# Keeping only the second parts of weight blocks in DRAM, with fewer steps in a layer norm and moved feed points, in a two-layer trunk on one core

## The chip, the cores and the metric

The kernel runs on one core of a Trainium2 chip. The metric is the device time of one execution in microseconds (us). The kernel before took 2473.21 us, the median of 3 runs (2469.9 to 2479.39).

## The reference

One inference step of a decoder trunk of two layers, for a prompt of 256 tokens and 8 samples of 4 tokens, 288 token columns in all, which share the weights. The model width is 2048. Cut to what is computed:

```python
for l in range(2):
    a = _rms(h, norm_mix_pre[l])
    if l % 2 == 0:   # pooling mixer | retention mixer, one input and one output projection
        y, ph, rs = _even_mixer(a, pos0, pool_hist[i], ret_state[i], w_in_even[i], w_pool[i],
                                s_pool[i], w_out_even[i])
    else:            # spatial gating mixer | Conformer convolution
        y, ch, sv = _odd_mixer(a, conv_hist[i], w_in_odd[i], sg_ln_g[i], sg_ln_b[i], sg_w[i], sg_b[i],
                               dw_w[i], dw_b[i], cv_ln_g[i], cv_ln_b[i], w_out_odd[i])
    h = h + _rms(y, norm_mix_post[l])
    f = _rms(h, norm_ffn_pre[l])
    f = jnp.square(jax.nn.relu(f @ w_up[l])) @ w_down[l]
    h = h + _rms(f, norm_ffn_post[l])
```

In the odd layer the four quarters of `a @ w_in` are u, v, a and gate. `v` takes a gelu and a layer norm, is mixed along the tokens and multiplied with gelu(u); `a * sigmoid(gate)` goes through a depthwise convolution of 31 taps, a second layer norm (`cv_ln`) and a silu. Both halves enter `w_out_odd`. Everything is float32; the outputs are the trunk's result for both groups and the new states.

## The kernel before

**Subs and groups.** Tokens lie along the free axis (288 columns), channels on partitions. All weights are streamed once, in 720 pieces of 256 rows by 512 columns, called subs (512 KB each, tile `raw`). A group is 512 output columns: 16 k-tiles in 8 subs (4 subs in the halves of `w_out_odd`). A group accumulates in four PSUM banks (`mm`). To keep float32 precision at the speed of a rounded type, each operand is split in two: ScalarE (ACT) rounds `raw` to `whi`, VectorE (DVE) computes `wlo = raw - whi`, and TensorE (PE) does three matmuls for each product: `whi` with the high part of the activations (`xhi`, `hidhi`), `wlo` with the same, and `whi` with their low part (`xlo`, `hidlo`). So a sub is 24 matmuls of 128x128 by 288 columns.

**The stages, in order of time.** Layer 0: the input projection of the even layer and its output projection (`wo_e`), up to 437 us; the MLP, to 1268 us, in four quarters of `up0` (4 groups) and `dn0` (4 groups). Layer 1: `w_in_odd` in eight groups in the order ga0, ga1, ga2, v0, v1, ga3, u0, u1 (ga: a and gate, together) from 1268 to 1506 us; `w_out_odd` in two halves (wo0, wo1) to 1640 us; the second MLP (`up1`, `dn1`) to the end.

**The feed.** Every sub takes a place in a list `feed`; `run()` (line 651) walks the subs, and at each emits what lets the next ones arrive: `emit_dma` loads `raw` (4 buffers) on the SP queue, `emit_hi` is the ACT rounding, `emit_lo` the DVE subtraction, each in a ring of `RING` = 3 pairs (`whi`, `wlo`) and some extra ones. `some(2)` lets two more places of the feed be split per sub. Every engine executes its instructions in the order in which they are emitted, so a `wlo` that waits for its `whi` holds up all that DVE has behind it. SP issues DMAs in order too.

**Kept subs.** In the MLP of layer 0 some places of the feed are jobs: a job loads, rounds and subtracts a sub of a later stage, in a pair of the same ring, and writes both parts to DRAM (`hik`, `lok`). The later sub is then of kind "kept" and reads both parts by DMA, with no work on ACT or DVE. `JOBS = (1, 5)` places two jobs in each group of the MLP but the first and the last. Sixty subs are kept: all 8 of ga0, 4 of each of the other seven groups of `w_in_odd`, 16 of `w_out_odd`, 8 of the first group of `up1`. `plan()` (line 537) pairs jobs and kept subs.

**Between the stages.** `boundary()` (line 371) closes a root mean square norm and opens the next: `last_sums` adds up squares on PE (`ms`), POOL and DVE make the factor (`sm`), PE spreads it over the partitions, `grow` scales `y` and adds it to `h`, and `xhi`, `xlo` are made from `h`. `keep_warm(n)` issues n matmuls whose result nobody reads. In the first group after a boundary the matmuls are ordered with k outside (`kouter`), and its results are parked (`defer`) until the norm's factor `rb` is there (`rest()`, line 689).

**Work beside the odd layer's matmuls.** The convolution runs in the background: taps on DVE (`cacc`), on ACT with a sum on POOL (`tap`, `conv`), one `bg_step` for each sub. When it is done, `conv_out` (line 1477) does the layer norm of the convolution (`layer_norm(..., by_pe=True)`, line 1342) and the silu, one step of the generator per sub, and makes `hidhi`, `hidlo` for the second half of `w_out_odd`. What is read out of PSUM at a group's end (`tmp<-mm`, `u<-mm`, `y<-mm`) stands in DVE's or ACT's order like all the rest, and PE needs these banks for the group after.

Of the kernel before, what the change touches and what calls it, by code (L numbers as in the profile page):

```python
# [178 lines left out]
def build(tc, ctx, I, O, C):  # L179
# [231 lines left out]
    def last_tiles(src, m):  # L411
# [61 lines left out]
    feed, pos, nraw, parts, kept = [], [], [], {}, {}  # L473
    RAW, RING = 4, 3
    JOBS = (1, 5)
# [16 lines left out]
    def emit_dma(p):  # L492
        kind, i = feed[p]
        if kind == "kept":
            return
# [16 lines left out]
    def emit_hi(p):  # L512
        kind, i = feed[p]
        hi, lo = parts[p] = ring_slot()
        if kind == "kept":
# [20 lines left out]
    def plan():  # L536

        todo = []
        where = {}
        at = 0  # L540
        for gi, g in enumerate(groups):
            for s in range(g.nsub):
                subs.append((g, s))
                if g.ahead and g.ahead(s):
                    todo.append(at + s)
            where[gi] = at
# [4 lines left out]
        ahead = set(todo)  # L551
        for i in range(len(subs)):
            pos.append(len(feed))
            feed.append(("kept" if i in ahead else "sub", i))
            if i in slots:
                feed.append(("job", slots[i]))
        n = 0
        for kind, i in feed:
            nraw.append(n)
            n += kind != "kept"  # L560
        nraw.append(n)

    def fetch():
        while W["dma"] < len(feed) and nraw[W["dma"]] < nraw[W["split"]] + RAW:
# [16 lines left out]
    def some(n):  # L581

        return min(W["split"] + n - 1, pos[W["now"]] + RING + W["extra"] - 1)
# [66 lines left out]
    def run():  # L650
# [3 lines left out]
        for i, (g, s) in enumerate(subs):  # L654
# [29 lines left out]
            if last:  # L684
                if g.defer:
# [44 lines left out]
    def ffn(layer, last):  # L730
        wu, wd = ("w_up", layer), ("w_down", layer)
        for q in range(4):
            for gm in range(4):
# [11 lines left out]
                def st_up(q=q, gm=gm):  # L745
                    if gm == 0:
# [4 lines left out]
                                  start=st_up, kouter=first, defer=first, jobs=() if last or first else JOBS,  # L751
                                  ahead=(lambda s: True) if last and first else None))
            for gm in range(4):
                def ev_dn(m, ps, gm=gm, q=q):
# [5 lines left out]
                    if q == 3:  # L760
# [3 lines left out]
                        else:  # L764
                            last_tiles(y(k), m)

                def fin_dn(q=q, gm=gm):
                    if q == 3 and gm == 3:
                        for m in range(4):
# [7 lines left out]
                                  jobs=() if last or (q == 3 and gm == 3) else JOBS))  # L777
# [331 lines left out]
    def even():  # L1109
# [35 lines left out]
        for gm in range(4):  # L1145
            def ev_o(m, ps, gm=gm):
# [5 lines left out]
                else:  # L1152
                    last_tiles(ps, m)
# [188 lines left out]
    def layer_norm(src, n, total, by_pe=False):  # L1342

        yield
        yield
# [25 lines left out]
        yield  # L1371
# [105 lines left out]
    def conv_out():  # L1477
# [4 lines left out]
        for k in range(8):  # L1482
# [6 lines left out]
            if k % 2 == 1:  # L1489
                yield  # L1490

    def odd():
# [9 lines left out]
        def ga(j):  # L1502
            def post_ga():
                if j == 1:
                    bg_drain(st_["setup"])
                if j == 0:
                    while "begun" not in Q:
# [9 lines left out]
                              ahead=lambda s: j == 0 or s % 2 == 1))  # L1517

        def vgrp(gm):
            def post_v():  # L1520
                if gm == 1:
# [5 lines left out]
                              post=post_v, ahead=lambda s: s % 2 == 1))  # L1527

        def ugrp(gm):
            def post_u():  # L1530
                if gm == 1:
                    bg_drain(st_["gate"])

                    def tail():
                        while any(c in bgs or c in fills for c in st_["conv"]):
# [7 lines left out]
                              start=start_u if gm == 0 else None, post=post_u, ahead=lambda s: s % 2 == 1))  # L1543
# [3 lines left out]
        for half in range(2):  # L1547
            for gm in range(4):
                def ev_o(m, ps, gm=gm, half=half):
# [5 lines left out]
                    else:  # L1555
# [4 lines left out]
                        else:  # L1560
                            last_tiles(y(k), m)

                def post_o(gm=gm, half=half):
                    if half == 0 and gm == 3:
                        for c in st_["conv"]:
# [13 lines left out]
                                  ahead=lambda s: s % 2 == 1))  # L1579
# [130 lines left out]
```

## Time and profile before

| | |
|---|---|
| median of 3 runs | 2473.21 us |
| profiled execution | 2476.82 us, span 2475.1 us |
| granted TensorE clock, mean | 0.988 |
| busy PE / DVE / ACT / POOL | 2420.7 (98%) / 1360.7 (55%) / 1090.6 (44%) / 251.9 us (10%) |
| DMA | 529.35 MB, mean 214 GB/s |

The profiled execution is 1.7 us longer than its span and 3.6 us longer than the median. Matmuls overlap: PE is busy 0.29 us with one, but starts one every 0.13 us. A busy PE is therefore no sign of progress by itself; matmuls per stretch are. All shares are means over stages that have different limits. In the rows, L162 is the helper through which DVE, ACT and POOL record their instructions, and L604 the matmuls of the subs.

### The profile page before, as it was taken

Reading aid. Unit: us, or ns where it says so; the run is one execution under the profiler, and the core shown is the slowest. Engines: PE = TensorE matmul, PEld = TensorE weight load, DVE = VectorE, ACT = ScalarE, POOL = GpSimd, SP = SyncE. Lnnn points to the kernel's source line nnn. Section 1 sums busy time; section 2 is a strip of 40 time slices with the busy share of each in tenths; the row PEclk is TensorE's granted clock in tenths of the full one; section 3 lists DMA queues with packets and bytes.
Section 4 is the critical chain, followed back from the end, with each engine's and each line's share of the span. In section 5 each row is a group of like instructions: output and inputs, shape, how many; then the busy total and the mean of one; then the engine's idle time right before and its main releaser. Section 6 shows DMA issues by size and latency. Waiting matters only on the chain.

```text
span 2475.1 us, 43388 instructions
## 1 busy us (share of the span) xinstructions
PE 2420.7 (98%) x17976; PEld 2386.2 (96%) x17976; DVE 1360.7 (55%) x1844; ACT 1090.6 (44%) x1567; POOL 251.9 (10%) x293
## 2 busy tenths in 40 slices
PE   9999999999999999999999999899999999999997
PEld 8899999999999999999999999899999999999997
DVE  5665564764455556555546976346434544544453
ACT  5343443554544455455434443435434434433442
POOL 0521111000000000000114750100000000000011
PEclk9999999999999999999999999999999999999998
DMA  7555464588888888888775656455555554545552
GB/s 253 164 185 181 159 206 160 181 280 296 289 289 297 279 295 290 294 288 293 261 254 211 246 200 219 179 196 190 168 164 168 163 169 161 172 162 170 165 166 92
DMA packets 146871, 529.35 MB, mean 214 GB/s; under 512 B 16809, under 2 KB 17849, under 8 KB 146649
## 3 DMA queue, kind: packets, MB, share of 16 engines
q1 hardware_dynamic: 142240, 511.81, 60.4%
q0 software_dynamic: 4288, 14.71, 1.8%
q8 instruction: 140, 2.29, 0.4%
q14 instruction: 59, 0.48, 0.1%
q10 hardware_dynamic: 144, 0.07, 0.0%
HBM read 453.68 MB, written 73.87 MB: 213 GB/s over the span
## 4 chain that ended last, share of the span: by engine, by line
PE 84%; DVE 6%; DMA 4%; ACT 3%; issue 2%; SPq 0%; POOL 0%; DVEq 0%; ACTq 0%; POOLq 0%
PE mm L604 81%; DVE wlo L162 2%; DVE cacc L162 2%; DMA raw<-in_wt 2%; DMA wlo<-lok 1%; ACT whi L162 1%; ACT tmp L162 1%; PE ms L313 1%; DMA lok<-wlo 1%; PE po L995 1%; DVE tmp L162 1%; PE ms L999 0%; DVE conv L162 0%; DVE yo L162 0%; PE ms L303 0%
## 5 line engine op out<-in xcount | busy, mean ns | idle before, releaser
L162 DVE TENSOR_TENSOR wlo<-raw,whi 128x1024 fp32r<-128x1024 f32 (+1 forms) x721 | 886.9, 1240 | 751.1 <-ACT whi L162 737.3
L162 ACT ACTIVATE whi<-raw 128x1024 fp32r<-128x1024 f32 (+1 forms) x721 | 755.1, 1057 | 1011.2 <-PE mm L604 892.1
L604 PE MATMUL mm<-xhi,wlo 128*128 128x288 f32 x3200 | 944.9, 297 | 11.3 <-DVE wlo L162 9.2
L604 PE MATMUL mm<-xhi,whi 128*128 128x288 f32 x3200 | 944.2, 297 | 10.3 <-DVE tmp L162 6.2
L604 PE MATMUL mm<-xlo,whi 128*128 128x288 f32 x3200 | 919.6, 296 | 0.0
L604 PE MATMUL mm<-hidhi,whi 128*128 128x288 f32 x2560 | 754.8, 296 | 6.8 <-ACT whi L162 3.2
L604 PE MATMUL mm<-hidhi,wlo 128*128 128x288 f32 x2560 | 757.6, 297 | 2.5 <-DMA wlo<-lok 1.7
L604 PE MATMUL mm<-hidlo,whi 128*128 128x288 f32 x2560 | 745.2, 296 | 0.0
L604 PEld LDWEIGHTS mm<-xhi,wlo 128*128 128x128 f32 x3200 | 605.4, 189 | 16.0 <-DVE wlo L162 13.2
L604 PEld LDWEIGHTS mm<-xhi,whi 128*128 128x128 f32 x3200 | 605.9, 189 | 13.3 <-issue 6.8
L604 PEld LDWEIGHTS mm<-xlo,whi 128*128 128x128 f32 x3200 | 595.8, 189 | 0.5 <-DVE xlo L162 0.5
L604 PEld LDWEIGHTS mm<-hidhi,whi 128*128 128x128 f32 x2560 | 485.3, 190 | 8.1 <-ACT whi L162 3.4
L604 PEld LDWEIGHTS mm<-hidhi,wlo 128*128 128x128 f32 x2560 | 485.4, 190 | 3.3 <-DMA wlo<-lok 2.1
L604 PEld LDWEIGHTS mm<-hidlo,whi 128*128 128x128 f32 x2560 | 480.3, 189 | 0.0
L162 POOL TENSOR_TENSOR acc<-acc,tmp 128x288 f32<-128x288 f32 x55 | 53.3, 970 | 1657.1 <-ACT tmp L162 1654.3
L162 DVE TENSOR_TENSOR y<-mm,y 128x288 f32<-128x288 f32 x112 | 50.9, 457 | 103.3 <-PE mm L604 103.3
L162 DVE SCALAR_TENSOR_TENSOR u<-mm,rb 128x288 f32<-128x288 f32 x120 | 54.3, 457 | 71.2 <-PE mm L604 71.2
L162 DVE SCALAR_TENSOR_TENSOR cacc<-gx,vecs,cacc 128x256 f32<-128x256 f32 x168 | 68.5, 478 | 0.0
L162 ACT ACTIVATE hidhi<-u 128x288 fp32r<-128x288 f32 x128 | 56.9, 445 | 4.1
L162 ACT ACTIVATE u<-u 128x288 f32<-128x288 f32 x128 | 55.3, 432 | 7.0 <-DVE u L162 6.9
L162 POOL TENSOR_TENSOR conv<-conv,tap 128x256 f32<-128x256 f32 x60 | 53.7, 895 | 13.6 <-ACT tap L162 10.0
L162 DVE TENSOR_TENSOR hidlo<-u,hidhi 128x288 fp32r<-128x288 f32 x128 | 49.7, 450 | 0.0
(180 smaller groups left out, 909.8 us busy)
## 6 DMA issues: line engine op xcount, KB each, us to landing
raw<-in_wt SPq DMA_DIRECT2D x719, 512.0 KB, 4.2
hik<-whi SPq DMA_DIRECT2D x60, 512.0 KB, 6.4
lok<-wlo SPq DMA_DIRECT2D x60, 512.0 KB, 7.1
whi<-hik SPq DMA_DIRECT2D x60, 512.0 KB, 4.4
wlo<-lok SPq DMA_DIRECT2D x60, 512.0 KB, 5.8
s0t<-in_state_ret POOLq DMA_DIRECT2D x24, 256.0 KB, 3.3
out<-s0t POOLq DMA_DIRECT2D x24, 256.0 KB, 3.4
out<-yo SPq DMA_DIRECT2D x8, 288.0 KB, 2.4
```

Of the source, the lines that this page charges most:

```text
L162: return call(*args, **kw)
L313: PE.matmul(P["sums"][:, t:t + 1], lhsT=a[:, c:c + 128], rhs=ones[:, 0:1], start=first and t == 0, stop=last and t == 2)
L604: PE.matmul(ps, lhsT=lhsT[:, k, c], rhs=rhs, start=s == 0 and k == 0 and which == 0, stop=s == g.nsub - 1 and k == 1 and which == 2)
L995: PE.matmul(po[gq:gq + 32, 0:256], lhsT=E["qdm"][:, hh, 32 * (b + i):32 * (b + i + 1)], rhs=s[:, i, :], start=False, stop=b >= 4, tile_pos ...
```

## The change

- Only the second part of a sub is kept. A job has buffers of its own (`jhi`, one; `jlo`, three) and writes `jlo` alone, 512 KB. The later sub (kind "lo") loads `raw` and rounds it on ACT as any other does, and its `wlo` comes from DRAM in place of the DVE subtraction.
- `JOBS` is (3, 5, 7), in other groups than before: none in the first two groups of `up0`, none in the last three of `dn0`. All eight groups of `w_in_odd` (64 subs) and the first group of `up1` (8 subs) are of kind "lo". For `w_out_odd` the new condition is written with `half`, a loop variable that the lambda reads when `plan()` runs, after the loop; it is 1 then, and no sub of `w_out_odd` is kept. The program so keeps 72 subs.
- `boundary()` feeds `some(2)` in place of the next sub alone.
- `last_sums` issues `keep_warm(1)` between its last two sums in the MLPs and in `w_out_odd`.
- `rest()` flushes waiting DVE work (`hidlo`) ahead of the parked results.
- `layer_norm` loses two steps where it is the convolution's, and `conv_out` has a step for every 4 channel tiles in place of 2.

```diff
@@ boundary
         rs = last_rs()
-        feed_hi(next_sub(W["now"]))
+        feed_hi(some(2))
@@ last_sums (last_tiles passes rest: True in dn and wo1, False in wo_e)
             sum_part(P.pop(("own", 2)))
+            if P.pop("rest"):
+                keep_warm(1)
             sum_part(P.pop(("own", 3)), last=True)
@@
-    JOBS = (1, 5)
+    JOBS = (3, 5, 7)
@@ emit_hi
-        hi, lo = parts[p] = ring_slot()
-        if kind == "kept":
-            for a, b in zip((hi, lo), kept[i]):
-                SP.dma_start(out=f(a), in_=b)
-        else:
-            A.activation(out=hi, in_=raws[p], func=AF.Copy)
-        if kind != "job":
-            his[i] = hi, lo
+        if kind == "job":
+            parts[p] = [W["pool"].tile([128, 2, 512], F32R, tag=t, name=t, bufs=n) for t, n in (("jhi", 1), ("jlo", 3))]
+            A.activation(out=parts[p][0], in_=raws[p], func=AF.Copy)
+            return
+        hi, lo = parts[p] = his[i] = ring_slot()
+        A.activation(out=hi, in_=raws[p], func=AF.Copy)
+        if kind == "lo":
+            SP.dma_start(out=f(lo), in_=kept[i])
@@ emit_lo
-        if kind != "kept":
-            V.tensor_tensor(out=lo, in0=raws.pop(p), in1=f(hi), op=SUB)
+        raw = raws.pop(p)
+        if kind != "lo":
+            V.tensor_tensor(out=lo, in0=raw, in1=f(hi), op=SUB)
         if kind == "job":
-            kept[i] = [dram.tile([128, 2, 512], F32, tag=f"{t}{i}", name=f"{t}k") for t in ("hi", "lo")]
-            W["out"] = [(b, a) for a, b in zip((hi, lo), kept[i])]
+            kept[i] = dram.tile([128, 2, 512], F32, tag=f"k{i}", name="kept")
+            W["out"] = [(kept[i], lo)]
@@ fetch, some
-        while W["dma"] < len(feed) and nraw[W["dma"]] < nraw[W["split"]] + RAW:
+        while W["dma"] < len(feed) and W["dma"] < W["split"] + RAW:
...
-        return min(W["split"] + n - 1, pos[W["now"]] + RING + W["extra"] - 1)
+        return min(W["split"] + n - 1, pos[min(W["now"] + RING + W["extra"], len(subs)) - 1])
@@ rest
                         yield from finish_pre(g.ready)
+                        flush()
@@ ffn
-  jobs=() if last or first else JOBS,
+  jobs=() if last or (q == 0 and gm < 2) else JOBS,
...
-  jobs=() if last or (q == 3 and gm == 3) else JOBS))
+  jobs=() if last or (q == 3 and gm > 0) else JOBS))
@@ layer_norm, in two places
-        yield
+        if not by_pe:
+            yield
@@ conv_out
-            if k % 2 == 1:
+            if k % 4 == 3:
                 yield
@@ odd (the groups of w_in_odd; then w_out_odd)
-  ahead=lambda s: j == 0 or s % 2 == 1))
+  ahead=lambda s: "lo"))
...
-  ahead=lambda s: s % 2 == 1))
+  ahead=lambda s: "lo" if half == 0 and s % 2 else None))
```

Three places show how the order moves. The first is DVE at the boundary between the even layer and the first MLP; `sm` is the norm's factor, `wlo` the subtraction of the feed, and `y<-y,ms`, `h<-h,y` the steps of `grow` that new activations wait for.

```order
 L162 TENSOR_SCALAR y_3774<-mm,vecs 128x288 x4
 L162 TENSOR_SCALAR sm_87<-ms 128x3
+L162 TENSOR_TENSOR wlo<-raw,whi 128x1024 x2
 L162 TENSOR_TENSOR y_3773<-y_3773,ms 128x288
 L162 TENSOR_TENSOR h<-h,y_3773 128x288
@@ -257,9 +258,7 @@
 L162 TENSOR_TENSOR h<-h,y_3774 128x576
 L162 SCALAR_TENSOR_TENSOR xlo<-h,vecs,xhi 128x288 x2
-L162 TENSOR_TENSOR wlo<-raw,whi 128x1024
 L162 TENSOR_TENSOR y_3774<-y_3774,ms 128x576
 L162 TENSOR_TENSOR h<-h,y_3774 128x576
```

Two subtractions stand ahead of the first step of `grow` now, and the ones among its later steps are gone.

The second is DVE in the groups ga2 and v0 of the odd layer: `tmp<-mm` reads a group's PSUM banks out, `cacc` are taps of the convolution. Before, from ga2's last subs to the read-out of v0:

```order
L162 TENSOR_TENSOR wlo<-raw,whi 128x1024
L162 TENSOR_REDUCE conv<-prod 128x32
L162 TENSOR_SCALAR conv<-conv,vecs 128x32
L162 SCALAR_TENSOR_TENSOR cacc<-gx,vecs,cacc 128x256 x9
L162 TENSOR_TENSOR wlo<-raw,whi 128x1024
L162 SCALAR_TENSOR_TENSOR cacc<-gx,vecs,cacc 128x256 x12
L162 SCALAR_TENSOR_TENSOR conv<-gx,vecs,cacc 128x256
L162 SCALAR_TENSOR_TENSOR cacc<-gx,vecs,cacc 128x256
L162 TENSOR_TENSOR conv<-cacc,conv 128x256
L162 TENSOR_TENSOR tmp<-mm,rb 128x288 x4
```

And now, at the like place:

```order
L162 TENSOR_REDUCE conv<-prod 128x32
L162 TENSOR_SCALAR conv<-conv,vecs 128x32
L162 SCALAR_TENSOR_TENSOR cacc<-gx,vecs,cacc 128x256 x25
L162 SCALAR_TENSOR_TENSOR conv<-gx,vecs,cacc 128x256
L162 SCALAR_TENSOR_TENSOR cacc<-gx,vecs,cacc 128x256
L162 TENSOR_TENSOR conv<-cacc,conv 128x256
L162 TENSOR_TENSOR tmp<-mm,rb 128x288 x4
```

No `wlo` stands among the taps of a group any more, and more taps stand ahead of a read-out; the last tap is emitted seven subs earlier than before.

The third is ACT in the first half of `w_out_odd`. `rl` is the factor of the convolution's norm, `tmp<-tmp,vecs` the silu, `hidhi` its rounding, and `y<-mm` the read-out of a group, which frees its banks. Before:

```order
L162 COPY rl<-ms 128x288
L162 ACTIVATE whi<-raw 128x1024
L162 ACT_TABLE_LOAD
L162 ACTIVATE tmp<-tmp,vecs 128x288
L162 ACTIVATE hidhi_16945<-tmp 128x288
L162 ACTIVATE tmp<-tmp,vecs 128x288
L162 ACTIVATE hidhi_16945<-tmp 128x288
L162 COPY y_16508<-mm 128x288 x4
```

And now, where the rows left out are two more silu pairs like the one shown, in each of two places:

```order
L162 COPY rl<-ms 128x288
L162 ACTIVATE whi<-raw 128x1024 x2
L162 ACT_TABLE_LOAD
L162 ACTIVATE tmp<-tmp,vecs 128x288
L162 ACTIVATE hidhi_16731<-tmp 128x288
...
L162 ACTIVATE whi<-raw 128x1024
L162 ACTIVATE tmp<-tmp,vecs 128x288
L162 ACTIVATE hidhi_16731<-tmp 128x288
...
L162 ACTIVATE whi<-raw 128x1024
L162 COPY y_16623<-mm 128x288 x4
```

All eight silu pairs stand ahead of the read-out of the group wo01, where two stood ahead of that of wo03 before.

## Rows read from the trace of the kernel before

**Rows 1.** Costliest groups: operation, count, busy us and mean ns, idle before it.

```profile
L162 DVE TENSOR_TENSOR wlo<-raw,whi 128x1024 fp32r<-128x1024 f32 (+1 forms) x721 | 886.9, 1240 | 751.1 <-ACT whi L162 737.3
L162 ACT ACTIVATE whi<-raw 128x1024 fp32r<-128x1024 f32 (+1 forms) x721 | 755.1, 1057 | 1011.2 <-PE mm L604 892.1
```

**Rows 2.** Stretches: length, busy PE, PEld, DVE, ACT, POOL, granted clock, DMA share, GB/s.

```profile
1350.00:1400.00 50.00, 47.04 (x345) 46.84 (x344) 48.56 (x89) 22.19 (x39) 38.82 (x40) 0.97 0.65 234
...
2000.00:2050.00 50.00, 50.00 (x381) 50.00 (x380) 22.12 (x24) 16.83 (x16) 0.00 (x0) 1.00 0.51 169
```

**Rows 3.** Matmuls of subs alone: stretch, length, PE busy, clock, DMA share, GB/s.

```profile
437.12:548.75 111.63, 106.39 (x768) 0.98 0.68 233
548.75:574.14 25.39, 25.39 (x194) 1.00 0.86 301
1268.30:1640.08 371.78, 326.78 (x2305) 0.95 0.61 222
1327.15:1505.61 178.46, 159.89 (x1154) 0.97 0.60 215
1533.60:1555.86 22.26, 16.61 (x98) 0.85 0.45 163
1555.86:1592.60 36.74, 30.06 (x195) 0.91 0.49 178
1355.66:1360.44 4.78, 4.78 (x24) 0.64 0.10 21
```

**Rows 4.** Waits of PE, 1250 to 1650 us: total, times, longest.

```profile
PE mm L604 <- DVE tmp L162: 8.3, 4, 3.0
...
PE mm L604 <- DMA wlo<-lok: 3.7, 4, 1.2
PE mm L604 <- ACT whi L162: 3.2, 1, 3.2
PE ms L1439 <- DVE mb L162: 2.9, 1, 2.9
```

**Rows 5.** Timeline of DVE ahead of v0: start, us, instruction, idle before.

```profile
1340.03 1.23 DVE L162 TENSOR_TENSOR wlo<-raw,whi 128x1024 fp32r<-128x1024 f32 x1 [4.20 <-ACT whi L162]
...
1355.07 1.18 DVE L162 TENSOR_TENSOR tmp<-mm,rb 128x288 f32<-128x288 f32 x3
```

**Rows 6.** Waits of DVE, 1327 to 1475 us: total, times, longest.

```profile
DVE wlo L162 <- ACT whi L162: 13.1, 5, 4.2
```

**Rows 7.** Groups of DVE, 1327 to 1506 us.

```profile
L162 DVE SCALAR_TENSOR_TENSOR cacc<-gx,vecs,cacc 128x256 f32<-128x256 f32 x153 | 62.3, 478 | 0.0
L162 DVE TENSOR_TENSOR wlo<-raw,whi 128x1024 fp32r<-128x1024 f32 x24 | 38.0, 1582 | 13.1 <-ACT whi L162 13.1
```

**Rows 8.** Timeline of PE, start of the fourth group of up0.

```profile
522.52 0.40 PE L604 MATMUL mm<-xhi,whi 128*128 128x288 f32 x1 [2.16 <-DVE u L162]
```

**Rows 9.** Timeline of ACT ahead of it.

```profile
519.78 1.06 ACT L162 ACTIVATE whi<-raw 128x1024 fp32r<-128x1024 f32 x1 [3.59 <-DMA raw<-in_wt]
```

**Rows 10.** Timeline of DVE at the boundary into the first MLP.

```profile
435.55 0.45 DVE L162 TENSOR_TENSOR y<-y,ms 128x288 f32<-128x288 f32 x1 [1.89 <-PE ms L303]
```

**Rows 11.** Groups of ACT, 1515 to 1590 us.

```profile
L162 ACT COPY y<-mm 128x288 f32<-128x288 f32 x16 | 6.1, 400 | 14.0 <-PE mm L604 14.0
L162 ACT ACTIVATE tmp<-tmp,vecs 128x288 f32<-128x288 f32 x8 | 5.0, 624 | 1.8 <-DVE tmp L162 1.8
L162 ACT ACTIVATE hidhi<-tmp 128x288 fp32r<-128x288 f32 x8 | 3.6, 444 | 0.3
...
L162 ACT ACT_TABLE_LOAD x1 | 1.3, 1283 | 1.7 <-DVE tmp L162 1.7
```

**Rows 12.** Timeline of PE, last sums ahead of the second MLP.

```profile
1630.47 0.81 PE L313 MATMUL ms<-cg,tmp 128*128 128x1 f32 x6
...
1633.27 1.44 PE L313 MATMUL ms<-cg,tmp 128*128 128x1 f32 x6 [0.52 <-ACT tmp L162]
```

**Rows 13.** Stretch of 8 us at the start of ga0, columns as in rows 2.

```profile
1268.00:1276.00 8.00, 7.47 (x52) 6.85 (x50) 7.72 (x14) 3.42 (x7) 0.12 (x1) 1.00 1.01 394
```

More of the change, by code (lines that the diff above doesn't have):

```diff
@@ L409, in scale_y, with last_tiles @@
         A.activation(out=y(k), in_=y(k), func=AF.Copy, scale=gain(which, layer, k))
-    def last_tiles(src, m):
+    def last_tiles(src, m, rest):
+        P["rest"] = rest
         if m < OWN:
@@ L472, in build @@
     subs = []
-    feed, pos, nraw, parts, kept = [], [], [], {}, {}
+    feed, pos, parts, kept = [], [], {}, {}
     RAW, RING = 4, 3
-    JOBS = (1, 5)
+    JOBS = (3, 5, 7)
     raws, his = {}, {}
@@ L493, in emit_dma @@
         kind, i = feed[p]
-        if kind == "kept":
-            return
         g, s = subs[i]
@@ L513, in emit_hi @@
         kind, i = feed[p]
-        hi, lo = parts[p] = ring_slot()
-        if kind == "kept":
-            for a, b in zip((hi, lo), kept[i]):
-                SP.dma_start(out=f(a), in_=b)
-        else:
-            A.activation(out=hi, in_=raws[p], func=AF.Copy)
-        if kind != "job":
-            his[i] = hi, lo
+        if kind == "job":
[6 more added lines that the diff above has]
+            SP.dma_start(out=f(lo), in_=kept[i])
     def emit_lo(p):
@@ L536, in plan @@
     def plan():
-        todo = []
+        todo, kinds = [], {}
         where = {}
@@ L543, in plan @@
                 subs.append((g, s))
-                if g.ahead and g.ahead(s):
+                kind = g.ahead(s) if g.ahead else None
+                if kind:
                     todo.append(at + s)
+                    kinds[at + s] = kind
             where[gi] = at
@@ L550, in plan @@
         slots = dict(zip(slots, todo))
-        ahead = set(todo)
         for i in range(len(subs)):
             pos.append(len(feed))
-            feed.append(("kept" if i in ahead else "sub", i))
+            feed.append((kinds.get(i, "sub"), i))
             if i in slots:
                 feed.append(("job", slots[i]))
[L557 to L561, printed above, removed]
     def fetch():
-        while W["dma"] < len(feed) and nraw[W["dma"]] < nraw[W["split"]] + RAW:
+        while W["dma"] < len(feed) and W["dma"] < W["split"] + RAW:
             emit_dma(W["dma"])
@@ L750, in ffn @@
                                   pre=(lambda: boundary(layer, 0)) if first else None,
-                                  start=st_up, kouter=first, defer=first, jobs=() if last or first else JOBS,
-                                  ahead=(lambda s: True) if last and first else None))
+                                  start=st_up, kouter=first, defer=first, jobs=() if last or (q == 0 and gm < 2) else JOBS,
+                                  ahead=(lambda s: "lo") if last and first else None))
             for gm in range(4):
@@ L764, in ev_dn @@
                         else:
-                            last_tiles(y(k), m)
+                            last_tiles(y(k), m, True)
                 def fin_dn(q=q, gm=gm):
@@ L1152, in ev_o @@
                 else:
-                    last_tiles(ps, m)
+                    last_tiles(ps, m, False)
                 V.tensor_scalar_mul(out=y(k), in0=ps, scalar1=gain(1, 0, k))
@@ L1370, in layer_norm @@
         yield
-        yield
+        if not by_pe:
+            yield
         pb = spread(rs)
@@ L1526, in vgrp @@
                               lambda m, ps: ev_v_odd(m, ps, gm), start=start_v_odd if gm == 0 else None,
-                              post=post_v, ahead=lambda s: s % 2 == 1))
+                              post=post_v, ahead=lambda s: "lo"))
         def ugrp(gm):
@@ L1542, in ugrp @@
             groups.append(Grp(w, [(512 * gm, 512)], list(range(KT)), xs, lambda m, ps: ev_u(m, ps, gm),
-                              start=start_u if gm == 0 else None, post=post_u, ahead=lambda s: s % 2 == 1))
+                              start=start_u if gm == 0 else None, post=post_u, ahead=lambda s: "lo"))
         for fn, i in ((ga, 0), (ga, 1), (ga, 2), (vgrp, 0), (vgrp, 1), (ga, 3), (ugrp, 0), (ugrp, 1)):
@@ L1560, in ev_o @@
                         else:
-                            last_tiles(y(k), m)
+                            last_tiles(y(k), m, True)
                 def post_o(gm=gm, half=half):
```

## The prediction, made before the run

> **What bounds the kernel now.** I read the page first: PE is busy nearly all the time, while DVE and ACT, which split every sub (1.24 us and 1.06 us each, [rows 1]), have most of their idle time in waits for one another or for PE. Busy shares don't say whether PE is at its pace, so I went to stretches of the span. From 2000 to 2050 us PE runs 381 matmuls, one every 131 ns; from 1350 to 1400 us only 345, and there DVE is busy 48.6 of 50 us [rows 2]. Then the subs' matmuls alone: in the first MLP 8 subs take 25.39 us, 3.174 us a sub [rows 3]. That is PE's own pace; nothing that shortens DVE, ACT or DMA is worth anything there, and the same holds for 740 us of the second MLP. In the odd layer, from 1268.30 to 1640.08 us, 96 subs take 371.8 us in place of 96 x 3.174 = 304.7 [rows 3]: 67 us are lost, and this is where the change works. From 1327 to 1506 us, 48 subs take 178.5 in place of 152.3: 26.1 us.
>
> What PE waits for there is the next view [rows 4]: 8.3 us in four waits for `tmp`, the read-out of a group's banks on DVE, and 2.9 us for `mb`, also DVE's. Each long wait has a second price: after it PE runs at a lower granted clock, and the first sub of v0 takes 4.78 us at a mean of 0.64 of full clock, 1.61 more than a sub at pace [rows 3]. The timeline of DVE shows why the read-out is late [rows 5]: at 1340.03 DVE had stood 4.20 us for a `whi`, with taps behind it that waited for nothing; at 1355.07 it begins the read-out that PE had wanted for 2.6 us. Five such stalls make 13.1 us [rows 6], and the 24 subtractions themselves 38 us, at 1.58 us each [rows 7]. DVE has no room left to make them good.
>
> **The change part by part.** The sums are made against the profiled execution, 2476.82 us, which is 3.6 us over the median of the runs shown.
>
> *DVE without subtractions in the odd layer.* Between 1327 and 1506 us the 24 `wlo` go, 38.0 us of work and 13.1 us of stalls [rows 6, 7]; the taps (153 x 0.41 us) stay and move ahead, some 40 to a group where some 30 were. A group so holds about 17 us of taps and 5 us of read-outs and sums, within 25.4: DVE reaches a read-out before PE does, whatever order the taps have. So the 11.2 us of waits go [rows 4], less 0.7 that the sums ahead of `mb` take on PE anyway, and the lower clock after four of them, 4 x 1.61 = 6.4. Together **-16.9 us**. What is late next is ACT: it gets 24 more `whi`, 25 us, in a stretch where it is half idle (22.2 of 50 us, [rows 2]). Bounds: -18.5 if the other small losses shrink too; -9 if ACT's bursts make half of the waits again.
>
> *The same in ga0 and ga1.* Waits for parts read by DMA (`lok`, 3.7 us, [rows 4], about half here) are of a kind that stays: on SP a `wlo` load now stands behind a `raw` that waits for the rounding of the sub four places back. Counted along the new order, a stall of about 2.7 us early in ga1 takes the place of 2.1. **+0.5**, between -2 and +3.
>
> *First MLP.* Jobs leave its first two groups. In its fourth group PE waits 2.16 us for a read-out [rows 8] that stands on DVE behind a subtraction, whose `whi` waited 3.59 us for a `raw` [rows 9]; with the lower clock after it the sub loses 3.5. The second group then moves 8 blocks of 512 KB in place of 14 (two job loads and four writes less), so the third starts with its buffers full; three jobs come into it all the same. I take **-3**, between -5 and 0. Deeper in the MLP a group moves 11 loads and 3 writes where it moved 10 and 4: the same 7.3 MB in 25.39 us that 301 GB/s at 0.86 share already carries [rows 3], and DVE and ACT stay below two thirds of a group. Nothing, between 0 and +5.
>
> *Boundary.* Two `wlo` of 1.24 us stand between `sm` and the first step of `grow`. DVE waits 1.89 us there for PE [rows 10], which hides the most: **+0.5** at the first boundary, between -0.5 and +1; at the other two they are `whi` on an idle ACT, nothing.
>
> *Convolution's norm and the silu.* Two places lose 9.6 us (22.26 against 4 x 3.174) and 11.3 us (36.74 against 8 x 3.174) [rows 3]: the norm's sums on PE with their lower clock, and ACT's pile of silu, after which PE waits 3.2 for `whi` and more for what follows. The norm only moves to a place a few subs earlier. The pile changes its form: behind `rl` ACT has two `whi` (2 x 1.06), a table load (1.28), four pairs of silu and rounding (4 x 1.07), a `whi`, four pairs, a `whi` and then the four copies that free wo01's banks (4 x 0.40) [rows 1, 11]: 15.7 us. `rl` comes no earlier than two subs, 6.3 us, after the step that starts it; PE wants the banks four subs and the sums later, 13.4. So 22.0 - 13.4 = 8.6 us of new wait and 1.6 of clock, for 11.3 that go. With the norm's sums about equal: **-0.5**, between -6 and +4. `w_out_odd` loses its 16 kept subs: 17 us of ACT and 20 of DVE over 135 us, in which DVE is half idle; hidden, but where the pile is.
>
> *The matmul within the sums.* PE waits 0.52 us ahead of the last six sums, which then take 1.44 us where six take 0.81 [rows 12]. One 288-column matmul fills the gap and holds the next up by some 0.2. Bounds +0.4 and -1.9 for each place, if the clock stays up behind it; I take **+0.2** at each of three, the nearest row being the gap's own. The Trainium skill (TensorE: Matmul & The Clock Gate, Part 1) says that the array's clock follows how busy it has been, so filler work keeps it; by that the sum would be -1.9 at two of the places. That a low clock follows a wait, the trace agrees; that one matmul suffices, no row shows.
>
> *First group of the second MLP.* One late load by the same chain as in ga1: **+0.5**, between 0 and +2.
>
> The sum is -16.9 + 0.5 - 3 + 0.5 - 0.5 + 0.6 + 0.5 = **-18.3**: 2458.5 in the profile's base, less 3.6, some 2455 us.
>
> **The rivals.** *The odd layer becomes bound by DMA.* All 64 subs of `w_in_odd` load 1.05 MB each, 330 GB/s at PE's pace. At the MLP's 301 GB/s a sub would take 3.48 us, 0.31 more, 64 times: +20, and the time would be 2475. For it: no long stretch of the trace moves more. Against it: 301 GB/s is a demand met at a share of 0.86 [rows 3], and 394 GB/s flowed over 8 us [rows 13]. The Trainium skill (DMA: Bandwidth & Descriptors, Specifications) gives some 358 GB/s as a core's limit to HBM; by it a sub would need 2.93 us and the rival falls, though with little left to catch up after a stall. The 8 us of [rows 13] lie above the figure.
>
> *The waits move to ACT.* `whi` now paces all subs, and taps, table loads and gelus stand before it. Half of the 16.9 comes back: 2463. For it: PE already waited 3.2 us for one `whi` [rows 4]. Against it: a `whi` is emitted two subs, 6 us, ahead of its use.
>
> *Slower.* The chain `whi` late, `raw` late, `wlo` load behind it late, makes a pile like that in wo1 at more places: 3.2 us for `whi`, the loads and two subs at half rate, about 9 us each. Beyond two piles more than counted the gain is used up; five give 2476.8 - 18.3 + 45 - 3.6 = 2500. The place would be the gelus and table loads of v0 to u1. Against it: these ran with ACT half idle.
>
> *More than forecast.* The new wait in `w_out_odd` doesn't come, since half of the silu pairs are done ahead of it, and the clock stays up in the sums: -6 and -3 more, 2446.
>
> **How the numbers follow.** Forecast 0.52 (2448 to 2462), more 0.15, moved to ACT 0.15, DMA 0.12, slower 0.06. A change of 0.5%, 12.4 us, is about what a measurement of this kernel can tell from none: faster is below 2460.8, slower above 2485.6. The first two cases and a part of the third lie below: 0.70; DMA and the rest between, 0.24; slower 0.06. For 8 in 10 the range goes from 2442 to 2474.
>
> **What would show it.** From 1327 to 1506 us: no wait of PE for `tmp` or `mb` over 1 us, and no granted clock of half after a group's start; 48 subs in about 162 us. Right for the new pile: a wait of PE for `y` of ACT, some 8 us, in the third group of the first half of `w_out_odd`. The DMA rival would show as waits of PE for `wlo<-kept` all over ga2 to u1 at a share near 1; the ACT rival as waits for `whi` with ACT busy; wrong boundary costs as more than 0.5 us between `sm` and `grow`. If the matmuls of the odd layer still take over 365 us, the forecast is wrong.

## The result, and the profile after

The changed kernel takes 2446.3 us, the median of 4 runs (2444.85 to 2448.25), against 2473.42 for the kernel before: a ratio of 0.9888, 95% interval 0.9868 to 0.9909. The forecast was 2455, with 2442 to 2474. The profiled execution has a span of 2443.4 us, 31.7 less than that of before; 27 of it is in the medians, since the profiled execution of before lay 3.4 us over its median and that of after about 1 under.

First the matmuls of the subs in the changed kernel, in the columns of [rows 3]: stretch, length, PE busy, clock, DMA share, GB/s. The stretches are up0, the whole odd layer, ga2 to u1, and the group wo01.

```profile
438.49:543.28 104.79, 103.21 (x768) 1.00 0.60 203
1261.18:1608.16 346.98, 316.31 (x2304) 0.98 0.71 254
1316.69:1479.07 162.38, 154.90 (x1155) 1.00 0.86 302
...
1500.98:1522.70 21.72, 13.10 (x99) 0.87 0.36 121
```

The odd layer takes 347.0 us where it took 371.8 [rows 3]. The 48 subs from ga2 to u1 take 162.4 (the forecast said 162) at a clock of 1.00, where they took 178.5 at 0.97. The group wo01 loses 9.0 us over its pace: that is the new pile of silu work. The waits of PE from 1240 to 1620 us, the answer to [rows 4]:

```profile
PE mm L601 <- ACT y L162: 8.2, 1, 8.2
PE mm L601 <- DMA wlo<-kept: 1.4, 1, 1.4
PE ms L1439 <- DVE mb L162: 0.5, 1, 0.5
PE mm L601 <- ACT whi L162: 0.2, 1, 0.2
```

The waits for `tmp` are gone, that for `mb` is 0.5, and one wait of 8.2 us for ACT's read-out is new, ahead of wo02; the 1.4 us for `wlo<-kept` lie in ga1. DVE shows the same from its side: from 1316 to 1460 us it waits for other engines, PE above all, and for no `whi`, the reverse of [rows 6].

```profile
DVE sm L162 <- PE ms L313: 9.4, 1, 9.4
DVE mb L162 <- PE ms L1439: 8.0, 5, 3.2
DVE tmp L162 <- PE mm L601: 6.8, 12, 2.0
DVE vg L162 <- ACT mean L162: 5.1, 1, 5.1
```

The same stretches as in [rows 2], 50 us each, in its columns, decide the rivals on DMA and on ACT:

```profile
1300.00:1350.00 50.00, 50.00 (x379) 49.60 (x379) 34.22 (x84) 28.86 (x45) 25.58 (x34) 1.00 0.93 341
1350.00:1400.00 50.00, 50.00 (x379) 49.89 (x378) 41.88 (x98) 29.85 (x49) 35.33 (x39) 1.00 0.95 332
```

DMA moves 332 to 341 GB/s at a share of 0.93 to 0.95 while PE keeps its pace of 379 matmuls; ACT has risen from 22 to 30 of 50 us. In these 100 us neither makes PE wait.

Where the span's 31.7 us went, place by place. A loss is the length of a stretch less its subs times 3.174 us. The stretch ahead of the first boundary, in which nothing was changed, took 0.5 us more.

| place | loss before | after | moved | forecast |
|---|---|---|---|---|
| up0, 32 subs | 10.1 | 3.2 | -6.8 | -3 |
| boundary into the first MLP | 6.5 | 7.5 | +0.9 | +0.5 |
| boundary into the odd layer and into the second MLP (sums) | 18.1 | 14.1 | -4.0 | +0.4 |
| ga0, ga1 | 8.1 | 4.7 | -3.3 | +0.5 |
| ga2 to u1, and the first sub of wo00 | 28.0 | 10.6 | -17.4 | -16.9 |
| the rest of wo00 to wo10 | 21.6 | 19.9 | -1.8 | -0.5 |
| first group of up1 | 0.3 | 0.7 | +0.4 | +0.5 |
| last group and the sums at the end | 20.0 | 19.8 | -0.2 | +0.2 |

### The profile page after: what moved, and what is told of

The parts are those of the page before. It is cut to its first block, busy times and chain, and to the rows that moved or that the text cites. A ratio compares the mean times of both kernels' runs of the same rounds, so it can differ in the third digit from the quotient of the medians.

```text
span 2443.4 us, 43554 instructions
## 1 busy us (share of the span) xinstructions
PE 2404.3 (98%) x17982; PEld 2372.2 (97%) x17982; DVE 1361.0 (56%) x1844; ACT 1163.5 (48%) x1639; POOL 239.3 (10%) x293
## 4 chain that ended last, share of the span: by engine, by line
PE 94%; DVE 2%; ACT 2%; issue 1%; DMA 0%; POOL 0%; SPq 0%; DVEq 0%; ACTq 0%; POOLq 0%
PE mm L601 91%; DVE wlo L162 1%; ACT tmp L162 1%; ACT whi L162 1%; PE ms L313 1%; PE po L993 1%; PE ms L997 0%; PE ms L303 0%; DVE yo L162 0%; DMA raw<-in_wt 0%; DMA wlo<-kept 0%; POOL sm L162 0%; PE ms L1439 0%; DVE e L162 0%; DVE tmp L162 0%
## 5 line engine op out<-in xcount | busy, mean ns | idle before, releaser
L162 DVE TENSOR_TENSOR wlo<-raw,whi 128x1024 fp32r<-128x1024 f32 (+1 forms) x649 | 795.1, 1230 | 632.0 <-ACT whi L162 630.8
L162 DVE TENSOR_TENSOR jlo<-raw,jhi 128x1024 fp32r<-128x1024 f32 x72 | 88.1, 1223 | 61.1 <-ACT jhi L162 49.3
L162 ACT ACTIVATE jhi<-raw 128x1024 fp32r<-128x1024 f32 x72 | 76.0, 1055 | 49.6 <-DMA raw<-in_wt 44.5
```

The lines of the kernel that those rows point to most:

```text
L162: return call(*args, **kw)
```

## The experiments

The theory: DVE's subtractions in the odd layer made the read-outs late, and their going carries the change; the fed boundaries, the filler in the sums and the moved jobs give the rest. The rivals: the steps of the norm and the fed boundaries carry it; or the taps that stand earlier, or the moved jobs, do.

**Two halves of the change.** One kernel has the kept second parts and the moved jobs alone, the other all the rest alone.

```diff
 e3_kept_alone, against the changed kernel (e4_rest_alone: the same lines the other way, in the kernel before)
-        feed_hi(some(2))
+        feed_hi(next_sub(W["now"]))
...
-            if P.pop("rest"):
-                keep_warm(1)
+            P.pop("rest")
...
-                        flush()
... (in two places)
-        if not by_pe:
-            yield
+        yield
...
-            if k % 4 == 3:
+            if k % 2 == 1:
                 yield
```

> Kept second parts and the moved jobs alone: no filler in the sums, boundary, norm, silu and flush as before. Theory A (the subtractions that leave DVE in the odd layer carry the change): from 1327 to 1506 us (its place in this kernel) 48 subs lose about 10 us over pace as in the changed kernel, against 26 before; with 3 back at the sums and the wait of 8.2 us ahead of wo02 smaller, since the silu pairs come two to a sub: 2443 to 2452 us. Theory B (the fewer steps of the norm and the fed boundaries carry it): over 2460 us.

> The kernel before with all of the change but the kept second parts and the moved jobs: filler in the sums, fed boundaries, fewer steps in the convolution's norm, silu in steps of four, flush. Theory A: the losses from ga2 to u1 stay at 26 us; the sums give 3 back, the first boundary costs 0.9, the silu pile changes by less than 3 either way: 2468 to 2474 us. Theory B (these carry it): below 2460 us.

Measured: 2455.28 us (ratio to before 0.9937, 0.9919 to 0.9954) and 2465.67 us (0.9972, 0.9962 to 0.9983); together 0.9% where the whole change gives 1.1%, a difference inside the intervals. The subs' matmuls of the kept parts alone, in up0, from ga2 to u1, and from wo00 to wo10:

```profile
439.24:545.96 106.72, 104.34 (x769) 1.00 0.59 200
1323.36:1485.73 162.37, 154.89 (x1154) 1.00 0.87 302
1485.73:1575.77 90.04, 73.22 (x483) 0.87 0.38 126
```

And of the rest alone:

```profile
439.49:547.82 108.33, 103.98 (x769) 0.99 0.67 232
1323.27:1503.02 179.75, 161.41 (x1154) 0.96 0.59 213
1503.02:1583.84 80.82, 71.53 (x481) 0.92 0.57 207
```

From ga2 to u1 the kept parts give all of the gain (162.4) and the rest gives none (179.8 against 178.5 before). From wo00 to wo10 it is the other way round. That stretch before, and in the changed kernel:

```profile
1505.61:1592.60 86.99, 74.21 (x481) 0.90 0.53 190
```

```profile
1479.07:1563.01 83.94, 70.34 (x482) 0.90 0.39 135
```

Against 87.0 us the kept parts alone make it 3.1 longer, the rest alone 6.2 shorter, and the two sum to the 3.1 of the whole change. So the forecast's -0.5 for that place looks like a sum of two larger terms; the traced execution of the first kernel was its slowest, 4.9 us over its median, so its share is the less sure. In up0 the halves show 4.9 and 3.3 of the 6.8, but the length of up0 differs by up to 3.5 us between executions of one program (shown under the feed, below).

Neither kernel met its theory A in time. The first ended over the range, between the two theories: the wait for a read-out was to be smaller, and it is 8.8 us, one group later. The second ended 2.3 us under the range: its loss from ga2 to u1 stayed (27.4 us), but the pile of silu, which was to change by less than 3, gave 6.2.

**The filler.**

```diff
-            if P.pop("rest"):
-                keep_warm(1)
+            P.pop("rest")
```

> The changed kernel without the one unread matmul between the last sums. Theory A (the filler keeps TensorE's clock up): the boundary into the odd layer, 7.07 us over pace in the changed kernel, goes back to some 7.9, that into the second MLP from 7.07 to some 9.4, with a granted clock below full there; in all +3.1, 2449.5 us. Theory B (the matmul fills a gap and nothing more; the boundaries are shorter because of the moved feed): both stay within 0.3 of 7.07, in all 2446 us.

Measured: 2448.75 us (ratio to before 0.9906, 0.9891 to 0.9922), and both boundaries at 8.3 us over pace in place of 7.06: 2.4 in all. The runs, 2445.04 to 2450.88 us, overlap those of the changed kernel, so the time by itself doesn't show the filler; the traces do. TensorE's sums ahead of the second MLP, first with the filler (the changed kernel), then without:

```profile
1602.43 0.72 PE L313 MATMUL ms<-cg,tmp 128*128 128x1 f32 x6
1603.02 0.73 PE L369 MATMUL ms<-acc,cg 128*128 128x288 f32 x2
1603.68 0.83 PE L313 MATMUL ms<-cg,tmp 128*128 128x1 f32 x6
1604.37 1.22 PE L369 MATMUL ms<-acc,cg 128*128 128x288 f32 x4
1605.70 0.85 PE L303 MATMUL ms<-cg,sm 128*128 128x128 f32 x6
1606.39 1.70 PE L369 MATMUL ms<-acc,cg 128*128 128x288 f32 x6
```

```profile
1607.29 0.83 PE L313 MATMUL ms<-cg,tmp 128*128 128x1 f32 x6 [0.52 <-ACT tmp L162]
1607.98 1.22 PE L369 MATMUL ms<-acc,cg 128*128 128x288 f32 x4
1609.31 1.29 PE L303 MATMUL ms<-cg,sm 128*128 128x128 f32 x6
1610.41 2.96 PE L369 MATMUL ms<-acc,cg 128*128 128x288 f32 x6
```

With it no wait is left ahead of the last six sums, and the spread takes 0.85 us; without it, 0.52 us of wait come back and the same matmuls take 1.29 and 2.96.

One trace on each side would be thin, since the clock within the sums is not the same in every execution: at the first boundary, which has no filler in any kernel, its mean is 1.00 in eight of the twelve kernels' traces and 0.70 to 0.79 in four. At the two places of the filler it is 0.67 to 0.82 in all six cases without it (three kernels), and with it 1.00 in fifteen cases and 0.67 to 0.81 in three (nine kernels). So theory A's mechanism holds, but not in every execution. A place without the filler loses 8.2 to 9.4 us, one with it and a full clock 7.1 (once 7.5). The kernel before, with 8.7 and 9.4, is at the upper end: there the clock fell one group of sums earlier [rows 12].

**The feed at the boundaries.**

```diff
-        feed_hi(some(2))
+        feed_hi(next_sub(W["now"]))
```

> The changed kernel with the boundary feeding the next sub alone, as before. Theory A (the two subtractions stand in the way of the first step of grow): the first boundary goes from 7.47 us over pace back to 6.55, the first group of up0 from 0.68 to some 2.2 since a subtraction is late there again; in all +0.6, 2447 us. Theory B (the moved feed shortened the other two boundaries): these go from 7.07 to 7.9 and 9.4, in all +3 to +4, 2450 us.

Measured: 2450.71 us (0.9915, 0.9899 to 0.9932), 4.4 over the changed kernel. The time is theory B's, but its mechanism is out: the other two boundaries stay at 7.06. Of theory A one half holds: the first group of up0 goes back to 2.0. But the feed works farther than I thought: ga0 goes from 0.7 to 2.5, and up1's first group from 0.7 to 1.2. Together that is 3.7 us, and the kernel with the kept parts alone, which feeds the next sub alone too, loses the same at these places (2.2, 2.3 and 1.2). The boundary itself did not go back to 6.55 but to 7.4: TensorE's sums ran at a lower clock in that execution (0.79).

The fourth group of up0 waits 1.5 us for its read-out again (its loss goes from 0.2 to 1.7), but that can't be put down to this edit. Three other kernels run the same program as the changed one up to there, and lose nothing (without the filler), 2.0 us (the kernel with work alone, below) and 3.6 us (one silu pair for each step, below) in that group; the kernel with the kept parts alone loses 0.6. So up0 loses 3.1 to 6.6 us in executions of one program.

**What makes the read-outs late.** The first kernel brings 28 subtractions back into the odd layer. The second keeps them away and gives DVE work without a wait at the same places.

```diff
 e5_every_second
-                              ahead=lambda s: "lo"))
+                              ahead=lambda s: "lo" if j == 0 or s % 2 else None))
 (and "lo" if s % 2 else None for v and u)
 e6_work_only, in emit_lo
+        elif subs[i][0].w[0] == "w_in_odd" and not subs[i][0].kouter and subs[i][1] % 2 == 0:
+            if "scr" not in Q:
+                Q["scr"] = Q["pool"].tile([128, 288], F32, tag="scr", name="scr")
+            for _ in range(3):
+                V.tensor_tensor(out=Q["scr"], in0=vecs[:, 0:288], in1=vecs[:, 100:388], op=SUB)
```

> The changed kernel with kept second parts only for ga0, every second sub of the other groups of the odd layer's input projection, and the first group of up1 (44 kept). 28 subtractions are back on DVE in the odd layer, in the places where the kernel before had them. Theory A (the subtractions and the stalls that they bring on DVE made the late read-outs): the waits of TensorE for tmp and mb come back, 48 subs from ga2 to u1 lose 22 to 27 us over pace against 10, in all 2460 to 2465 us. Theory B (the gain there came from the taps that stand earlier, or from the jobs): the loss stays below 15, 2446 to 2451 us.

> The changed kernel with three VectorE subtractions of 128x288, between constants and into a tile that nobody reads, at each of the 28 places where the run before this one puts a subtraction back: DVE's work without its wait for whi. Theory A1 (the in-order stalls make the read-outs late): the loss from ga2 to u1 stays at 10 to 14 us, 2446 to 2451 us. Theory A2 (the work itself fills DVE): it goes back to over 20, 2457 to 2465 us.

Measured: 2469.49 us (0.9982, 0.9970 to 0.9993) and 2469.57 us (0.9981, 0.9972 to 0.9991). The subs' matmuls from ga2 to u1, with the subtractions back, and with the work alone:

```profile
1320.44:1502.47 182.03, 160.78 (x1155) 0.96 0.59 208
```

```profile
1319.06:1501.18 182.12, 160.31 (x1154) 0.97 0.78 270
```

Both lose some 29.7 us, a little more than the kernel before and more than the 22 to 27 that I gave the first; both times lie over the ranges as well (2460 to 2465 and 2457 to 2465). The gain from ga2 to u1 so comes from the DVE work that went: the second kernel has the jobs and the kept parts of the changed one, and the gain is gone. And it takes no stall for `whi`: work that waits for no other result does the same.

The taps' half of theory B needs a second look, since the convolution (`conv_all`) places its taps by the work that DVE has, and in both kernels they went back to where they stood before. In five of the six groups the changed kernel has more taps ahead of the group's read-out than the kernel before (39, 41, 40, 34 and 26 in ga2, v0, v1, u0 and u1, against 29, 30, 31, 22 and 24), and yet the loss of these groups fell from 22.3 to 8.9 us. There the earlier taps are more work ahead of a read-out and can't be what helps. In ga3 alone it has none in place of 29, and no run parts that from the subtractions (a loss of 3.9 us before, 1.2 after).

The two groups of DVE between 1316 and 1500 us, of the one and of the other kernel:

```profile
L162 DVE TENSOR_TENSOR wlo<-raw,whi 128x1024 fp32r<-128x1024 f32 x25 | 42.0, 1679 | 10.0 <-ACT whi L162 9.8
```

```profile
L162 DVE TENSOR_TENSOR scr<-vecs 128x288 f32<-128x288 f32 x69 | 49.8, 721 | 1.6
```

42.0 us of work with 10.0 of stalls, and 49.8 with 1.6, are about the same DVE time, so the test doesn't part a microsecond of stall from one of work. Part of both is time beside POOL: a subtraction alone takes 1.23 us, one of the 128x288 kind 0.46 (the last section comes back to it). It fits that the sum of work and stall decides, on an engine that takes its work in order: DVE is busy 155 and 169 of the 182 us, where it is busy 128 of 162 in the changed kernel. No run varies the one with the other held.

**The new wait in w_out_odd.** ACT in the changed kernel, ahead of the copies that free wo01's banks (the other two pairs of each four are left out):

```profile
1507.26 1.28 ACT L162 ACT_TABLE_LOAD   x1
1509.10 0.63 ACT L162 ACTIVATE tmp<-tmp,vecs 128x288 f32<-128x288 f32 x1 [0.55 <-DVE tmp L162]
...
1513.15 1.04 ACT L162 ACTIVATE whi<-raw 128x1024 fp32r<-128x1024 f32 x1
1517.34 0.63 ACT L162 ACTIVATE tmp<-tmp,vecs 128x288 f32<-128x288 f32 x1 [3.14 <-DVE tmp L162]
...
1521.32 1.04 ACT L162 ACTIVATE whi<-raw 128x1024 fp32r<-128x1024 f32 x1
1522.27 1.28 ACT L162 COPY y<-mm 128x288 f32<-128x288 f32 x4
```

That is the order that the forecast counted through, with two waits for DVE's `tmp`, 0.55 and 3.14 us, that its count left out. The next kernel puts one pair into each step, and the one after it also keeps the second parts of 8 subs of `w_out_odd`, which the change's condition was written for and misses:

```diff
 e8_one_silu
-            if k % 4 == 3:
-                yield
+            yield
 e9_silu_eighty, besides
-  ahead=lambda s: "lo" if half == 0 and s % 2 else None))
+  ahead=lambda s, half=half: "lo" if half == 0 and s % 2 else None))
```

> The changed kernel with one silu pair for each step of the convolution's output in place of four. Theory A (the wait of 8.2 us ahead of wo02 is ACT's pile of eight pairs ahead of the copies that free wo01's banks): ahead of these copies stand two pairs, six fewer at 1.07 us and the subtractions' waits; the wait falls below 1.5 us and the slow sub after it goes: 2435 to 2439 us. Theory B (the copies wait for something else, the norm's factor or the roundings): the wait stays over 5 us, 2443 to 2447 us.

> The run before this one with the condition of w_out_odd's groups bound to its half, so that 80 subs are kept: 8 jobs more in the first MLP, 16 subs of the first half of w_out_odd with a second part kept where their number is odd. Theory A: DVE is not what bounds there, so no change beyond 1 us from the run before, and at most a late load or two: 2435 to 2440 us. Theory B (DVE's subtractions hold the silu's second parts up): 2 to 4 us less.

Measured: 2445.14 us (0.9886, 0.9871 to 0.9901), no gain that can be told from the changed kernel, and 2437.96 us (0.9858, 0.9843 to 0.9873). The first has theory B's time and a part of theory A's mechanism: the wait of 8.2 fell to 1.1, but one of 3.0 came in the next group. Its waits for `y` from 1480 to 1560 us, and the subs' matmuls in up0 and from wo00 to wo10:

```profile
PE mm L601 <- ACT y L162: 4.2, 2, 3.0
```

```profile
440.48:548.65 108.17, 104.80 (x769) 0.98 0.61 207
1484.51:1565.31 80.80, 71.25 (x482) 0.92 0.42 139
```

From wo00 to wo10 it gains 3.1 us on the changed kernel; up0, where nothing was edited, took 3.4 us more in this execution. DVE in that kernel, one step of the silu:

```profile
1524.52 1.23 DVE L162 TENSOR_TENSOR wlo<-raw,whi 128x1024 fp32r<-128x1024 f32 x1 [2.12 <-ACT whi L162]
1525.66 0.45 DVE L162 TENSOR_TENSOR hidlo<-tmp,hidhi 128x288 fp32r<-128x288 f32 x1
1526.03 0.45 DVE L162 TENSOR_TENSOR tmp<-conv,rl 128x288 f32<-128x288 f32 x1
1528.60 1.23 DVE L162 TENSOR_TENSOR wlo<-raw,whi 128x1024 fp32r<-128x1024 f32 x1 [2.12 <-ACT whi L162]
```

and ACT in the same step:

```profile
1526.52 0.63 ACT L162 ACTIVATE tmp<-tmp,vecs 128x288 f32<-128x288 f32 x1 [2.03 <-DVE tmp L162]
1527.18 0.45 ACT L162 ACTIVATE hidhi<-tmp 128x288 fp32r<-128x288 f32 x1
1527.53 1.04 ACT L162 ACTIVATE whi<-raw 128x1024 fp32r<-128x1024 f32 x1
```

From one `wlo` to the next is 4.08 us, over a sub's 3.17. It is a circle: `wlo` waits for `whi`, `tmp` stands behind `wlo` on DVE, the silu waits for `tmp`, and the next `whi` stands behind the silu on ACT. Neither engine is full; their two orders pace each other. With every second `wlo` taken from DRAM the circle stands only at every second sub, and PE waits for no read-out there at all. The subs' matmuls from wo00 to wo10 take

```profile
1482.88:1554.47 71.59, 66.19 (x483) 0.98 0.59 205
```

us, in place of 83.9 in the changed kernel and 80.8 in the one with a silu pair for each step. My theory A for that run, that DVE doesn't bind there, was wrong: the time lies in the range that it named, but 7.2 us under the run before it, where A allowed 1 and B 2 to 4.

**The boundary's cost, and the norm's sums.** Two more edits of that kernel:

```diff
 e10_lo_later
         if P["fin"]:
             P["fin"]()
-        feed_lo()
...
         second(0)
         second(1)
+        feed_lo()
 e11_sum_adds (two silu pairs for each step, and)
-        yield from layer_norm(lambda k: cv[:, k, :], SGC, Q["csum"], True)
+        yield from layer_norm(lambda k: cv[:, k, :], SGC, Q["csum"], False)
```

> The kernel with one silu pair for each step and 80 kept subs, with the two subtractions of a boundary put behind its first two steps of grow. Theory A (at the first boundary POOL's power step of the norm's factor took 1.78 us in place of 0.86, because VectorE subtracts at the same time): it goes back to 0.86, the wait of TensorE of 1.0 us for sm goes, the boundary loses 6.5 us over pace in place of 7.45; in all 1 us less, 2437 us, less whatever a later subtraction costs the first group of up0. Theory B (the first steps of grow behind the subtractions on VectorE are what is late): the boundary gets shorter, POOL's step stays at 1.78.

> 80 kept subs, two silu pairs for each step, and the convolution's norm with its sum of squares added up on POOL and summed once by TensorE, in place of 48 one-column matmuls. Theory A (these matmuls and the low clock behind them are the 7 to 9 us that wo00 loses): wo00 loses under 3 us over pace; 2431 to 2435 us if the silu is done in time. Theory B (the loss is the clock's, whatever TensorE does there, or the later steps make a new wait ahead of wo10): 2436 to 2442 us.

Measured: 2439.86 us (0.9858, 0.9840 to 0.9876) and 2432.39 us (0.9831, 0.9817 to 0.9846). POOL at the first boundary, in the changed kernel, and with the subtractions moved behind the first two steps of `grow`:

```profile
434.19 1.78 POOL L162 TENSOR_TENSOR sm<-sm,cg 128x3 f32<-128x3 f32 x1 [6.32 <-DVE sm L162]
```

```profile
434.23 0.86 POOL L162 TENSOR_TENSOR sm<-sm,cg 128x3 f32<-128x3 f32 x1 [6.32 <-DVE sm L162]
```

POOL's power step of 3 columns takes 0.92 us longer while DVE subtracts, as theory A had it, and the wait of PE for `sm` at that place goes. It gains nothing: in that execution the clock fell within the sums (the spread took 1.32 us), so that the boundary loses 7.4 us still, and up0's first group loses 4.1 in place of 0.7, with a wait of 2.0 us for `xhi` that comes 5.6 us after its start. What POOL's step costs the traces of all kernels tell: where the clock stayed at 1.00, the boundary loses 6.5 us with the step at 0.86 (two kernels) and 7.5 with it at 1.78 (six); where it fell, 7.4 (two) and 8.9 (two).

With the sum of squares off TensorE the subs' matmuls from wo00 to wo10, in the same view, need

```profile
1482.74:1550.76 68.02, 65.06 (x483) 1.00 0.61 217
```

us, 3.6 less than in the kernel with 80 kept subs, at a full clock; wo00 loses 0.5 where it lost 7.4, and the time lies in theory A's range. The edit also brings the norm's two steps back and puts two silu pairs into a step, but neither explains wo00: the kernel with the kept parts alone has the two steps and loses 11.3 us there, and the silu comes after it. This is the fastest of all the kernels, 14 us under the changed one.

## Why the prediction was right

The time, 2446.3 us, is 8.7 under the forecast and lies in its range, though just under the band of 2448 to 2462 that the forecast itself covered. The main step was right in mechanism and size; the rest of the gain came from terms that were too small or had the wrong sign, all to the same side.

*DVE without subtractions* (-16.9): -17.4. Mechanism and size held: no wait for `tmp`, 0.5 for `mb`, clock 1.00, 48 subs in 162.4 us where 162 was said. That DVE reaches a read-out before PE is seen in its waits for PE; only one order of the taps was run, so that it holds for any is not shown.

*ga0 and ga1* (+0.5): -3.3, the wrong sign. The stall counted along the order came at half its size (1.4 us for `wlo<-kept`, 2.7 forecast), and the waits of before went together with the slow subs behind them. With `some(2)` at the boundary ga0 has its first parts in time and loses 0.7; without it, it loses 2.5.

*First MLP* (-3): -6.8 in this execution; by the other executions of the same program there, 3.5 to 7.0. In the second and third group the moved jobs save 1.6 us in every trace, and in the fourth, which lost 4.0, all but 0.0 to 3.6. So the mechanism held, and how far the size was off is open. The fed boundary gave up0's first group 1.3, and that term was missing: I had priced the boundary's edit as a cost alone.

*Boundary* (+0.5): +0.9 in that place, by another way. The first step of `grow` was not held up by DVE (it still waited 0.53 us for PE); POOL's `sm` took 0.92 us longer, and at a full clock that is the whole difference, 6.5 to 7.5 us.

*Convolution's norm and silu* (-0.5): -1.8. The new wait was put at 8.6 us and came at 8.2, at the place named, with 1.6 for the clock forecast and 2.2 found. The place and the cause were right, the closeness of the size was luck: from the first `whi` behind `rl` to the first copy the count has 14.5 us, and ACT took 17.5, with 3.7 of waits for DVE; but `rl` was there 9.3 us ahead of the time at which PE wanted the banks, where the count has 7.1. Also, 8.6 and 1.6 for 11.3 make -1.1, and the step gave no reason for the -0.5 in its place.

*The matmul within the sums* (+0.6): -4.0 over the two places, 2.4 of it the filler's by the run without it; the rest lies in how early the clock fell in the execution of before. The third place, at the end, moved by -0.2, less than it differs between kernels (19.4 to 20.7). This is the worst-sized term, and its sign was wrong. I took the nearest row, the gap, for the price, and left the clock to the other end of the range. By the Trainium skill (TensorE: Matmul & The Clock Gate, Part 1) I had -1.9 for each of two places, and the trace of after sides with it, as most of the others do: the last unread matmuls of the second place take 1.70 us, and took 2.69 before.

*The rivals.* DMA carried 341 GB/s over 50 us without a wait; "moved to ACT" shows as 0.2 us; of the piles of "slower" none came beyond the one that was counted. The figure that I gave from the Trainium skill (DMA: Bandwidth & Descriptors, Specifications), some 358 GB/s, lies above the 341 GB/s at a share of 0.93, so these 50 us agree with it but don't test it; the 8 us of [rows 13] lie over it. "More than forecast" came nearest, 2446 us, but only one of its two causes did: the clock stayed up in the sums, while the new wait in `w_out_odd` came in full.

## What to carry to other kernels

On an engine that works in order, count the whole time between two read-outs that the tensor engine waits for, stalls and work together; taking work away there pays twice, in the wait and in the low clock behind it. When two engines hand parts to each other in turns, follow the circle through both orders: its length paces the kernel though neither engine is full. An edit that moves work into a wait can cost little where it stands and pay in the groups behind, so price it there too. And before a place's gain is put down to an edit, look at that place in other executions of the same program: up0's fourth group lost from 0.0 to 3.6 us with nothing changed.

## What the hardware showed that I had not expected

POOL and DVE hold each other up. POOL's 128x3 step took 0.86 us alone and 1.78 beside a DVE subtraction of two operands in SBUF. In the other direction, two stretches of DVE in the kernel with work alone, each with three subtractions of 128x288:

```profile
1349.87 1.48 DVE L162 TENSOR_TENSOR scr<-vecs 128x288 f32<-128x288 f32 x3
...
1355.53 2.89 DVE L162 TENSOR_TENSOR scr<-vecs 128x288 f32<-128x288 f32 x3
```

The same work took 1.48 us beside no more than two copies of 128x30 on POOL, and 2.89 beside three additions of POOL from 1355.52 on. It looks like turns and not like sharing: each of the three subtractions ends 0.32 us after one of the additions, and at the first boundary POOL's step ends 0.72 us after the DVE subtraction that began 0.16 us ahead of it. The Trainium skill (GPSIMD Engine Reference, 1. Specifications) says that GpSimd shares its SBUF interfaces with VectorE, with contention for DVE instructions of two SBUF inputs; the step on POOL and the subtractions agree. The taps agree as well: they read `gx` from SBUF and `cacc` from PSUM, one SBUF tensor only, and they stayed at 0.48 us each in the kernels before, after and with work alone.

One unread matmul in a gap of 0.52 us kept TensorE's granted clock at 1.00 through the sums that followed in fifteen of eighteen cases; without it the clock fell in six of six, and the spread of the factor took 1.26 to 1.49 us in place of 0.85.
